# Layer 0's modulation vectors: 32 x 32 block transposes on VectorE and four column-tiled products in place of four TensorE transposes

## The chip, the cores and the metric

One core of a Trainium2 chip runs the whole program, in one launch. The metric is the device time in microseconds; smaller is better. Three runs of the kernel before took 3101.84, 3100.47 and 3102.82 us, median 3101.84.

## The reference

Two transformer layers of width 2048 work on 256 latent tokens and 256 context tokens in fp32. Layer 0 mixes tokens by four pooling windows, layer 1 by neighbourhood attention; both have a gated feed-forward part with a three-tap convolution. Every sub-layer is modulated by vectors that come from one row vector each for the latents (`c`) and the context (`c_ctx`):

```
silu_c, silu_cc = jax.nn.silu(c), jax.nn.silu(c_ctx)
for i in range(DEPTH):
    ml = (silu_c @ w_mod[i] + b_mod[i]).reshape(B, 6, 1, D)
    mc = (silu_cc @ w_mod[i] + b_mod[i]).reshape(6, 1, 1, D)
    a_lat = modulate(rms_norm(h, norm1_g[i]), ml[:, 0], ml[:, 1])
    ...
    h = h + ml[:, 2] * y_lat
    h = h + ml[:, 5] * conv_ffn(modulate(rms_norm(h, norm2_g[i]), ml[:, 3], ml[:, 4]),
                                ffn_w_gate[i], ffn_w_up[i], ffn_conv_w[i], ffn_conv_b[i], ffn_w_down[i])
```

`w_mod` is 2048 x 12288 per layer: a large weight for a product with two rows.

## The kernel before

Channels lie on partitions and tokens along the free axis. A large product is taken three times in a one-pass fp32 form: weights and activations are each split into a high and a low part (ACT rounds, DVE subtracts, L143 and L145), and PE adds high x high, high x low and low x high.

**Layer 0's modulation (`mod_pe`, L187 to L206).** The 12288 columns are 24 chunks of 512. A chunk is loaded in four pieces of 1 MB, two tiles each (L192, issued at L127 on SP's queue). For a piece, four products (L193) with 32-column weights `sc` stand at the four column positions of the array, `tile_position=(0, 32 * j)`, and all 16 of a chunk add up in the one PSUM bank of tag `m`. Then position j holds a quarter of the sum over input channels for both streams, as rows, and it must become columns with the four quarters added: ACT copies the bank to `modev` (L198), PE turns it by four 128 x 128 transposes against `ident` into a bank of tag `d` (L203, tile `modt`, under high priority), DVE adds the four quarters (L205, via the view `by_row`), and `finish_mod` adds the bias (L181) and, for scales, the norm's gain (L183).

**The late shift (`partial`, L514 to L569).** In layer 0 the feed-forward products of the first eight column tiles are begun per channel group g before the second norm is known. What the shift vector adds to them is computed from the same weight tiles by small column-tiled products (L528, tiles `pwg` and `pwu`, 16 sets of eight), which also come out as rows and are turned the same way: ACT copy `peg`/`peu` (L532), four transposes `ptg`/`ptu` (L561), a DVE reduction (L564 or L568) and, for g > 0, an addition into `wsh` (L569).

**What sets the order.** The Python text gives dependencies and priorities; a scheduler in the build places the instructions of each engine's queue by its own timeline, so that pieces of a chunk are spread among the feed-forward products of `partial` (L545 to L547, tiles `cg` and `cu`) and of the pooling mixer (L484 to L486, tile `pm`). `need` and `between` only say when a piece is written down. Each engine then works through its queue strictly in order. Loads take turns in a ring of tiles (`stage`): six of its own, and more that `lend` adds or takes away. The bank of tag `m` exists once, so chunk n + 1 cannot begin before chunk n's bank has been read; tag `d` has three.

The whole of this lies in the first 455 us. Later, layer 1's vectors are made on DVE (`mod_pairs`), which already uses 32 x 32 block transposes from SBUF (L251) and the constant `quad` (four stacked 32 x 32 identities, four times side by side).

Of the kernel before, what the change touches and what calls it, by code (L numbers as in the profile page):

```python
# [10 lines left out]
F32 = mybir.dt.float32  # L11
F32R = mybir.dt.float32r
AF = mybir.ActivationFunctionType
ALU = mybir.AluOpType
AX = mybir.AxisListType
PSUM = bass.MemoryType.PSUM

P = 128
# [39 lines left out]
def kernel(ctx: ExitStack, tc: tile.TileContext, xT, cxT, wmod, wg, wu, wd, wp,  # L58
                         wq, wv, wo, vec, cc, rope, inv, strips, out):
    nc = tc.nc  # L60
    main = ctx.enter_context(tc.tile_pool(name="main", bufs=1))
# [30 lines left out]
    ident = main.tile([P, P], F32, name="ident")  # L92
# [61 lines left out]

    both = (0, 1)

    def by_row(ps):

        return ps.rearrange("p (i j c) -> p i c j", i=4, j=4)[:, :, 0:2, :]

    def quarter_sum(x, n, name):

# [5 lines left out]

    def finish_mod(l, ch, streams, src):

        mt = src[0] if len(src) == 1 else main.tile([P, 4, 2], F32, name=f"modT{l}_{ch}")
        n = len(streams)
        which, q = divmod(ch, 4)

        def dup(name, a):
            return V(name)[:, a : a + 8].rearrange("p (i s) -> p i s", s=2)[:, :, 0:n]

        bias = dup(f"bm_{l}", 8 * ch)
        for b, v in enumerate(src):
            own = slice(32 * b, 32 * b + 32) if len(src) > 1 else slice(0, P)  # L180
            nc.vector.tensor_tensor(mt[own, :, 0:n], v, bias[own], op=ALU.add)  # L181
        if which in (1, 4):
            nc.vector.scalar_tensor_tensor(mt[:, :, 0:n], mt[:, :, 0:n], 1.0, dup(f"g{1 if which == 1 else 2}_{l}", 8 * q),  # L183
                                           op0=ALU.add, op1=ALU.mult)
        modT[l, ch] = mt

    def mod_pe(l, ch, sc, pool):  # L187

        ps = bank("m", f"mod{l}_{ch}")
        for g in range(4):  # L190
            ts = load(lambda a, b: wmod[l, ch, g, :, a:b], 2048, f"wm{l}_{ch}_{g}")
            for j in range(4):  # L192
                nc.tensor.matmul(ps[32 * j : 32 * j + 32, :], sc[:, 4 * g + j, :],  # L193
                                 ts[j // 2][0][:, 512 * (j % 2) : 512 * (j % 2) + 512],
                                 start=(g == 0), stop=(g == 3), tile_position=(0, 32 * j))
            if g == 3:
                ev = pool.tile([P, 512], F32, tag="t2", name=f"modev{l}_{ch}")
                nc.scalar.copy(ev, ps)  # L198
            yield
        with tc.high_priority():  # L200
            p2 = bank("d", f"modt{l}_{ch}")
            for i in range(4):
                nc.tensor.transpose(p2[:, P * i : P * i + P], ev[:, P * i : P * i + P], ident)  # L203
        r = main.tile([P, 4, 2], F32, name=f"modT{l}_{ch}")
        nc.vector.tensor_reduce(out=r, in_=by_row(p2), axis=AX.X, op=ALU.add)  # L205
        finish_mod(l, ch, both, [r])  # L206

    def mod_pairs(todo, ring):

# [113 lines left out]
    with ExitStack() as ph0:  # L323
# [62 lines left out]
        with ExitStack() as phs:  # L386
# [123 lines left out]
            def partial(g, sh, between):  # L510

                step = 0
                for fa in range(0, NS, 4):
                    for q, (nm, wsrc) in enumerate((("g", wg), ("u", wu))):  # L514
# [3 lines left out]
                        for j in range(4):  # L518
                            f = fa + j
                            between(2 * step)  # L520
                            if j == (3 if fa == 0 and q == 0 else 0):
                                need(20 * g + 21)
                                assert g in READY
                                pw = bank("d", f"pw{nm}{g}_{fa}")
                                for i in range(4):
                                    for jj, (t, n) in enumerate(ts):
                                        t3 = t.rearrange("p (f c) -> p f c", c=512)
                                        nc.tensor.matmul(pw[32 * i : 32 * i + 32, 256 * jj : 256 * jj + 256], sh[:, i, :],  # L528
                                                         t3[:, :, P * i : P * i + P], start=True, stop=True,
                                                         tile_position=(0, 32 * i))  # L530
                                ev = f0.tile([P, 512], F32, tag="t2", name=f"pe{nm}{g}_{fa}")
                                nc.scalar.copy(ev, pw)  # L532
                            if f >= NC:
                                if g == 0:
                                    HELD[f, q] = bank("gu", f"c{nm}_{f}")
                                ps = HELD[f, q]
                                first, final = g == 0, g == 3
                            else:
                                ps = bank("d", f"c{nm}{g}_{f}")
                                first = final = True  # L540
                            hi, lo = parts[j // 2]
                            for i in range(4):
                                c = 512 * (j % 2) + P * i
                                xh, xl = flat(A[4 * g + i][:, 0]), flat(A[4 * g + i][:, 1])
                                nc.tensor.matmul(ps, hi[:, c : c + P], xh, start=(first and i == 0), stop=False)  # L545
                                nc.tensor.matmul(ps, hi[:, c : c + P], xl, start=False, stop=False)
                                nc.tensor.matmul(ps, lo[:, c : c + P], xh, start=False, stop=(final and i == 3))  # L547
                                if i == 1:
                                    between(2 * step + 1)
                            step += 1  # L550
                            if f >= NC:
                                continue
                            if g == 0:
                                if q == 0:
                                    PART[f] = act_tile(f"part{f}", F32)
                                nc.scalar.copy(PART[f][:, q], ps)
                            else:
                                nc.vector.tensor_tensor(PART[f][:, q], PART[f][:, q], ps, op=ALU.add)
                        p2 = bank("d", f"pt{nm}{g}_{fa}")
                        for i in range(4):  # L560
                            nc.tensor.transpose(p2[:, P * i : P * i + P], ev[:, P * i : P * i + P], ident)  # L561
                        w_ = wsh[:, q, fa : fa + 4, :]
                        if g == 0:
                            nc.vector.tensor_reduce(out=w_, in_=by_row(p2), axis=AX.X, op=ALU.add)  # L564
                            continue
                        t_ = f0.tile([P, 512], F32, tag="t2", name=f"pu{nm}{g}_{fa}")[:, 0:8]
                        t_ = t_.rearrange("p (f s) -> p f s", s=2)
                        nc.vector.tensor_reduce(out=t_, in_=by_row(p2), axis=AX.X, op=ALU.add)  # L568
                        nc.vector.tensor_tensor(w_, w_, t_, op=ALU.add)  # L569
            lend(range(4, KT))  # L570
            mix = mixer(0)
            for n in STEPS:
# [659 lines left out]
```

## Time and profile before

| what | before |
|---|---|
| runs | 3101.84 us median (3100.47 to 3102.82) |
| the profiled execution's own time | 3103.48 us |
| its span | 3101.7 us (1.8 us lie around it) |
| PE, DVE, ACT, POOL busy | 98%, 62%, 44%, 27% |
| HBM | 180 GB/s mean, 376 and 333 GB/s in the first two of 40 slices |
| layer 0's modulation and late shift | 19.7 to 455 us |
| their instructions that the change touches | 40 ACT copies, 160 transposes, 40 reductions, 12 additions |

The profile counts an engine as busy while an instruction of it is in flight, and matmuls overlap each other, so a busy PE says only that PE had no hole. A group of rows gives the busy time of all, the mean of one, and the idle time just before. In a timeline row the first number is the start, the second the length up to the end of the row's last instruction; the next row's start tells when the next one went in. An fp32 product has two rows in the trace, one for each of its passes: four products at L193 are eight records.

### The profile page before, as it was taken

To read this page: it belongs to the slowest core of one execution; us is meant where nothing else is said; L and a number is where in the kernel's file an instruction comes from. 1 tells how busy PE (TensorE), PEld (TensorE's weight loads), DVE (VectorE), ACT (ScalarE), POOL (GpSimd) and SP (SyncE) were. 2 spreads that over 40 slices of the span, in tenths; PEclk is the share of its full clock that TensorE was granted. 3 is DMA by queue.
4 is the path that set the end of the run, shared out by engine and by line. 5 is a ranking of instruction groups with operands and counts; after the bars stand their busy time and mean duration, and the time that the engine had idled before them with its cause. 6 is when DMAs were issued, how large, how long until landed. Compare 5 with 4: busy or idle time off the path is not lost.

```text
span 3101.7 us, 40819 instructions
## 1 busy us (share of the span) xinstructions
PE 3030.0 (98%) x15082; PEld 2414.3 (78%) x15082; DVE 1932.6 (62%) x2748; ACT 1373.2 (44%) x2219; POOL 826.1 (27%) x823
## 2 busy tenths in 40 slices
PE   6999899999999999999999999999999999999998
PEld 2565558888888888888888788878788888888887
DVE  4445674285765848567485665564777666666666
ACT  3333454333233332323334444343545666656665
POOL 2011213213031230302213000000002466556665
PEclk9999999999999999999999999999999999999999
DMA  9978573264846657475573333332345565555563
GB/s 376 333 271 306 177 246 102 89 217 149 251 141 206 198 162 247 133 225 171 182 226 118 102 113 106 102 114 96 111 153 179 177 196 188 192 189 185 179 195 117
DMA packets 177927, 559.70 MB, mean 180 GB/s; under 512 B 17600, under 2 KB 22208, under 8 KB 177728
## 3 DMA queue, kind: packets, MB, share of 16 engines
q1 hardware_dynamic: 177728, 557.10, 55.0%
q8 instruction: 119, 1.95, 0.3%
q14 instruction: 80, 0.66, 0.1%
HBM read 554.93 MB, written 2.10 MB: 180 GB/s over the span
## 4 chain that ended last, share of the span: by engine, by line
PE 94%; DMA 2%; DVE 2%; POOL 1%; ACT 1%; issue 0%; SPq 0%; DVEq 0%; ACTq 0%; POOLq 0%
PE g L766 5%; PE u L766 5%; PE d L657 5%; PE d L659 5%; PE d L658 5%; PE d L813 4%; PE u L631 4%; PE u L632 4%; PE u L633 4%; PE g L631 4%; PE g L633 4%; PE g L632 4%; PE mod L193 3%; PE u L769 3%; PE g L769 3%; PE d L817 2%
## 5 line engine op out<-in xcount | busy, mean ns | idle before, releaser
L670 POOL TENSOR_TENSOR hl<-hl,dy 128x256 f32<-128x256 f32 x160 | 149.0, 931 | 958.6 <-ACT dy L669 957.3
L828 POOL TENSOR_TENSOR hl<-hl,dy 128x256 f32<-128x256 f32 x320 | 331.5, 1069 | 188.4 <-ACT dy L826 186.1
L241 DVE SCALAR_TENSOR_TENSOR macc<-wm,sc,macc 128x512 f32<-128x512 f32 (+1 forms) x360 | 325.2, 935 | 68.6 <-DMA wm<-wmod 67.6
L669 ACT ACTIVATE dy<-d,modT 128x256 f32<-128x256 f32 x320 | 133.5, 470 | 196.8 <-PE d L659 195.5
L193 PE MATMUL mod<-wm,sc 128*32 128x512 f32 x768 | 134.6, 618 | 26.6 <-DMA wm<-wmod 26.5
L670 POOL TENSOR_TENSOR hc<-hc,dy 128x256 f32<-128x256 f32 x160 | 126.0, 787 | 0.0
L145 DVE TENSOR_TENSOR wd_2l<-wd,wd_2h 128x1024 fp32r<-128x1024 f32 (+1 forms) x44 | 53.9, 1229 | 112.8 <-ACT wd_2h L143 112.8
L826 ACT ACTIVATE dy<-d,modT 128x512 f32<-128x512 f32 x160 | 104.4, 683 | 42.7 <-PE d L817 41.2
L915 POOL TENSOR_TENSOR rk<-rk,rp 128x256 f32<-128x256 f32 x16 | 13.2, 826 | 365.4 <-DVE rk L914 309.8
L145 DVE TENSOR_TENSOR wd_3l<-wd,wd_3h 128x1024 fp32r<-128x1024 f32 (+1 forms) x44 | 52.0, 1202 | 80.6 <-ACT wd_3h L143 80.6
L145 DVE TENSOR_TENSOR wd_1l<-wd,wd_1h 128x1024 fp32r<-128x1024 f32 (+1 forms) x44 | 53.7, 1224 | 58.6 <-ACT wd_1h L143 58.6
L466 POOL TENSOR_TENSOR pf<-ws,inv 128x256 f32<-128x256 f32 x32 | 27.7, 886 | 222.4 <-DVE ws L461 154.7
L193 PEld LDWEIGHTS mod<-wm,sc 128*32 128x32 f32 x768 | 23.6, 110 | 81.0 <-issue 59.4
L143 ACT CAST wd_1h<-wd 128x1024 fp32r<-128x1024 f32 (+1 forms) x44 | 45.2, 1029 | 79.8 <-PE u L632 50.6
L145 DVE TENSOR_TENSOR wd_0l<-wd,wd_0h 128x1024 fp32r<-128x1024 f32 (+1 forms) x44 | 54.6, 1247 | 40.7 <-ACT wd_0h L143 40.6
L1004 ACT ACTIVATE sb<-sb,nm 128x512 f32<-128x512 f32 x64 | 46.1, 721 | 64.4 <-DVE nm L1000 63.2
L143 ACT CAST wd_0h<-wd 128x1024 fp32r<-128x1024 f32 (+1 forms) x44 | 45.3, 1031 | 57.9 <-PE u L766 29.1
L792 DVE TENSOR_TENSOR actb<-sgb,actb 128x256 fp32r<-128x256 f32 x43 | 52.3, 1216 | 27.0 <-ACT actb L791 27.0
L657 PE MATMUL d<-act,wd_2h 128*128 128x512 f32 x172 | 68.0, 395 | 0.0
L658 PE MATMUL d<-act,wd_2h 128*128 128x512 f32 x172 | 67.9, 395 | 0.0
L657 PE MATMUL d<-act,wd_3h 128*128 128x512 f32 x172 | 67.9, 395 | 0.0
L657 PE MATMUL d<-act,wd_0h 128*128 128x512 f32 x172 | 67.9, 395 | 0.0
(1752 smaller groups left out, 9286.1 us busy)
## 6 DMA issues: line engine op xcount, KB each, us to landing
wm<-wmod SPq DMA_DIRECT2D x384, 512.0 KB, 6.1
wd<-wd SPq DMA_DIRECT2D x168, 512.0 KB, 4.4
wg<-wg SPq DMA_DIRECT2D x156, 512.0 KB, 4.6
wu<-wu SPq DMA_DIRECT2D x156, 512.0 KB, 4.5
wv<-wv SPq DMA_DIRECT2D x32, 512.0 KB, 3.9
wk<-wq SPq DMA_DIRECT2D x32, 512.0 KB, 4.0
wq<-wq SPq DMA_DIRECT2D x32, 512.0 KB, 3.7
wo<-wo SPq DMA_DIRECT2D x32, 512.0 KB, 4.4
```

The costliest lines, as they stand in the source:

```text
L145: eng.tensor_tensor(lo[:, :n], t[:, :n], hi[:, :n].bitcast(F32), op=ALU.subtract)
L193: nc.tensor.matmul(ps[32 * j : 32 * j + 32, :], sc[:, 4 * g + j, :], ts[j // 2][0][:, 512 * (j % 2) : 512 * (j % 2) + 512], start=(g == 0) ...
L241: nc.vector.scalar_tensor_tensor(acc[s], v, sc2[:, k, s : s + 1], acc[s], op0=ALU.mult, op1=ALU.add)
L631: nc.tensor.matmul(ps, hi[:, c : c + P], xh, start=(k == 0), stop=False)
L632: nc.tensor.matmul(ps, hi[:, c : c + P], xl, start=False, stop=False)
L633: nc.tensor.matmul(ps, lo[:, c : c + P], xh, start=False, stop=(k == KT - 1))
L657: nc.tensor.matmul(ps, hi[:, o : o + P], xh, start=(i == 0), stop=False)
L658: nc.tensor.matmul(ps, hi[:, o : o + P], xl, start=False, stop=False)
L670: nc.gpsimd.tensor_tensor(h_of(s)[:, k, :], h_of(s)[:, k, :], y[:, s], op=ALU.add)
L766: nc.tensor.matmul(ps, hi[:, c : c + P], flat(B[k]), start=(k == 0), stop=False)
L769: nc.tensor.matmul(ps[:, T:], lo[:, c : c + P], B[k][:, 0], start=False, stop=(k == KT - 1))
L828: nc.gpsimd.tensor_tensor(hl[:, k, :], hl[:, k, :], y[:, q], op=ALU.add)
```

## The change

Both turns are made another way. `turned` lets DVE read the PSUM bank itself and turn its sixteen times four 32 x 32 blocks by one instruction (`nc.vector.transpose` on 128 x 512), so the ACT copy goes. After that the two wanted rows of a quarter are columns on the quarter's own 32 partitions, one block of 32 channels behind the other, in SBUF. `by_row` adds the four quarters with products against `quad[:, 0:32]`: four of them with 8 columns each (four blocks, two streams), of which the one for block b of every 128 channels stands at column position 32 b. They replace the transposes and the reduction. The bias is added by DVE straight from that PSUM bank; for the late shift DVE copies it or adds it to `wsh`. The high priority of the turn is gone. Besides, `mod_pe` writes the products of pieces 0 and 1 down together after the load of piece 1, and those of 2 and 3 after the load of piece 3: eight in a row in the text.

```
+    def turned(ps, pool, name):
+        t = pool.tile([P, 512], F32, tag="t2", name=name)
+        nc.vector.transpose(t, ps)
+        return t.rearrange("p (i b r) -> p b i r", b=4, r=32)[:, :, :, 0:2]
+
+    def by_row(x, name):
+        ps = bank("d", f"{name}s")[:, 0:8].rearrange("p (i s) -> p i s", s=2)
+        for b in range(4):
+            nc.tensor.matmul(ps[32 * b : 32 * b + 32], quad[:, 0:32], x[:, b], start=True, stop=True,
+                             tile_position=(0, 32 * b))
+        return ps
...
-            for j in range(4):
-                nc.tensor.matmul(ps[32 * j : 32 * j + 32, :], sc[:, 4 * g + j, :],
-                                 ts[j // 2][0][:, 512 * (j % 2) : 512 * (j % 2) + 512],
-                                 start=(g == 0), stop=(g == 3), tile_position=(0, 32 * j))
+            if g % 2 == 0:
+                t0 = ts
+            for k, tt in () if g % 2 == 0 else ((g - 1, t0), (g, ts)):
+                for j in range(4):
+                    nc.tensor.matmul(ps[32 * j : 32 * j + 32, :], sc[:, 4 * k + j, :],
+                                     tt[j // 2][0][:, 512 * (j % 2) : 512 * (j % 2) + 512],
+                                     start=(k == 0), stop=(k == 3), tile_position=(0, 32 * j))
             if g == 3:
-                ev = pool.tile([P, 512], F32, tag="t2", name=f"modev{l}_{ch}")
-                nc.scalar.copy(ev, ps)
+                x = turned(ps, pool, f"modev{l}_{ch}")
             yield
-        with tc.high_priority():
-            p2 = bank("d", f"modt{l}_{ch}")
-            for i in range(4):
-                nc.tensor.transpose(p2[:, P * i : P * i + P], ev[:, P * i : P * i + P], ident)
-        r = main.tile([P, 4, 2], F32, name=f"modT{l}_{ch}")
-        nc.vector.tensor_reduce(out=r, in_=by_row(p2), axis=AX.X, op=ALU.add)
-        finish_mod(l, ch, both, [r])
+        finish_mod(l, ch, both, [by_row(x, f"modt{l}_{ch}")])
...
-                                ev = f0.tile([P, 512], F32, tag="t2", name=f"pe{nm}{g}_{fa}")
-                                nc.scalar.copy(ev, pw)
+                                x = turned(pw, f0, f"pe{nm}{g}_{fa}")
...
-                        p2 = bank("d", f"pt{nm}{g}_{fa}")
-                        for i in range(4):
-                            nc.tensor.transpose(p2[:, P * i : P * i + P], ev[:, P * i : P * i + P], ident)
-                        w_ = wsh[:, q, fa : fa + 4, :]
+                        w_, v = wsh[:, q, fa : fa + 4, :], by_row(x, f"pt{nm}{g}_{fa}")
                         if g == 0:
-                            nc.vector.tensor_reduce(out=w_, in_=by_row(p2), axis=AX.X, op=ALU.add)
-                            continue
-                        t_ = f0.tile([P, 512], F32, tag="t2", name=f"pu{nm}{g}_{fa}")[:, 0:8]
-                        t_ = t_.rearrange("p (f s) -> p f s", s=2)
-                        nc.vector.tensor_reduce(out=t_, in_=by_row(p2), axis=AX.X, op=ALU.add)
-                        nc.vector.tensor_tensor(w_, w_, t_, op=ALU.add)
+                            nc.vector.tensor_copy(w_, v)
+                        else:
+                            nc.vector.tensor_tensor(w_, w_, v, op=ALU.add)
```

Three places show what the scheduler makes of it. In the names, `mod_9` and `wm_9_2_0` are chunk 9 and its piece 2 (columns 0 or 1024), the last number is a buffer's; lines of the changed kernel differ by a few (L206 is the old L193, L160 the block transpose, L167 the four small products, L191 the old L181).

The first is PE's queue at the last two pieces of chunk 9, among products of `partial`. Before:

```order
L193 MATMUL mod_9_897<-wm_9_2_0_956,sc 32x512 x2
L546 MATMUL cg_964<-Ad_567,wcg_4h_866 128x512
L547 MATMUL cg_964<-Ad_567,wcg_4l_867 128x512
L545 MATMUL cg_964<-Ad_572,wcg_4h_866 128x512
L193 MATMUL mod_9_897<-wm_9_2_1024_958,sc 32x512 x2
```

and now:

```order
L206 MATMUL mod_9_890<-wm_9_2_0_949,sc 32x512 x2
L206 MATMUL mod_9_890<-wm_9_2_1024_951,sc 32x512 x2
L550 MATMUL cg_995<-Ad_559,wcg_4h_860 128x512
L206 MATMUL mod_9_890<-wm_9_3_0_981,sc 32x512 x2
L551 MATMUL cg_995<-Ad_559,wcg_4h_860 128x512
```

Piece 2 now stands together, but pieces 2 and 3, eight products in the text, are still apart, and piece 3 is split. Over the whole queue up to the first L631 the column-tiled products stand in 95 unbroken runs before and in 85 now. The 384 products of L193 need 122 sets of up to four different column positions before and 126 now; 96 would do if every four stood together.

The second is DVE's queue at the end of chunk 8, the chunk before the first mixer's products. Before:

```order
L461 TENSOR_TENSOR ws_369<-pad_200 128x2x271
L470 TENSOR_TENSOR ph_361<-pf_357,ph_361 128x512
L467 TENSOR_TENSOR pf_371<-pf_371,pad_200 128x512
L205 TENSOR_REDUCE modT_8_405<-modt_8_400 128x8
L181 TENSOR_TENSOR modT_8_405<-modT_8_405,vt 128x8
```

and now:

```order
L467 TENSOR_TENSOR ws_363<-pad_200 128x2x271
L145 TENSOR_TENSOR wp0l_381<-wp_1024_374,wp0h_380 128x1024
L476 TENSOR_TENSOR ph_355<-pf_351,ph_355 128x512
L473 TENSOR_TENSOR pf_365<-pf_365,pad_200 128x512
L160 STREAM_TRANSPOSE modev_8_396<-mod_8_291 128x512
L476 TENSOR_TENSOR ph_369<-pf_365,ph_369 128x512
L191 TENSOR_TENSOR modT_8_403<-modt_8s,vt 128x8
```

What reads the bank of chunk 8 was a copy on ACT; it is now on DVE, behind the fourth `pf` (L467 before, L473 now).

The third is DVE's queue at the end of chunk 10, in the third mixer. Before:

```order
L461 TENSOR_TENSOR ws_1720<-ws_1720 128x2x265
L453 SCALAR_TENSOR_TENSOR py_1770<-hl,modT_6_1639,rs_194 128x256
L453 SCALAR_TENSOR_TENSOR py_1770<-hc,modT_6_1639,rs_194 128x256
L145 TENSOR_TENSOR wp2l_1863<-wp_1024_1856,wp2h_1862 128x1024
L205 TENSOR_REDUCE modT_10_1758<-modt_10_1753 128x8
```

and now:

```order
L467 TENSOR_TENSOR ws_1700<-ws_1700 128x2x265
L145 TENSOR_TENSOR wp2l_1844<-wp_1024_1837,wp2h_1843 128x1024
L160 STREAM_TRANSPOSE modev_10_1729<-mod_10_1627 128x512
L459 SCALAR_TENSOR_TENSOR py_1749<-hl,modT_6_1624,rs_194 128x256
L459 SCALAR_TENSOR_TENSOR py_1749<-hc,modT_6_1624,rs_194 128x256
```

The block transpose stands behind both splits of `wp2`, and the pair `py` has gone behind it.

More of the change, by code (lines that the diff above doesn't have):

```diff
@@ L155 @@
     both = (0, 1)
-    def by_row(ps):
-        return ps.rearrange("p (i j c) -> p i c j", i=4, j=4)[:, :, 0:2, :]
+    def turned(ps, pool, name):
[8 more added lines that the diff above has]
+        return ps
     def quarter_sum(x, n, name):
@@ L169, in finish_mod @@
     def finish_mod(l, ch, streams, src):
-        mt = src[0] if len(src) == 1 else main.tile([P, 4, 2], F32, name=f"modT{l}_{ch}")
+        mt = main.tile([P, 4, 2], F32, name=f"modT{l}_{ch}")
         n = len(streams)
```

## Prediction

> **What bounds the kernel now.** First the page: which engine has no holes, and what the chain that ended last is made of.
>
> ```profile
> span 3101.7 us, 40819 instructions
> PE 3030.0 (98%) x15082; PEld 2414.3 (78%) x15082; DVE 1932.6 (62%) x2748; ACT 1373.2 (44%) x2219; POOL 826.1 (27%) x823
> ...
> PE 94%; DMA 2%; DVE 2%; POOL 1%; ACT 1%; issue 0%; SPq 0%; DVEq 0%; ACTq 0%; POOLq 0%
> ```
>
> PE sets the end. Whatever shortens PE's queue before its last layer-0 shift is kept to the end, since behind it the work is the same. Next, the windows (us, then busy time of PE, PEld, DVE, ACT, POOL, clock, DMA share, GB/s) for the stretch in which the changed instructions lie:
>
> ```profile
> 20.00:60.00 40.00, 31.39 (x133) 9.77 (x130) 19.41 (x40) 10.46 (x18) 7.73 (x9) 0.91 1.03 408
> 60.00:100.00 40.00, 38.55 (x201) 20.52 (x200) 12.61 (x23) 17.59 (x34) 5.68 (x8) 1.00 0.97 350
> 100.00:350.00 250.00, 248.47 (x1392) 152.65 (x1391) 130.49 (x221) 91.13 (x160) 40.73 (x47) 1.00 0.77 278
> 350.00:455.00 105.00, 93.40 (x460) 48.42 (x459) 66.74 (x124) 45.16 (x87) 19.73 (x15) 0.97 0.70 240
> ```
>
> Up to 60 us the loads bound (408 GB/s, DMA share 1.03); from 60 to 350 us PE has 3 us of holes in 290; behind that 11.6 us in 105. DVE has time left everywhere, on the mean. So the change is worth what it takes from PE's own queue, plus or minus holes.
>
> **What it removes from PE.** The timeline of PE gives the prices:
>
> ```profile
> 167.56 0.60 PE L203 MATMUL modt<-ident,modev 128*128 128x128 f32 x4
> 168.09 1.92 PE L193 MATMUL mod<-wm,sc 128*32 128x512 f32 x16
> 169.95 0.66 PE L561 MATMUL ptu<-ident,peu 128*128 128x128 f32 x4
> 170.53 1.92 PE L193 MATMUL mod<-wm,sc 128*32 128x512 f32 x16
> ...
> 196.24 0.39 PE L546 MATMUL cu<-Ad,wcu_0h 128*128 128x512 f32 x1
> 196.47 0.39 PE L547 MATMUL cu<-Ad,wcu_0l 128*128 128x512 f32 x1
> 196.79 1.05 PE L193 MATMUL mod<-wm,sc 128*32 128x512 f32 x4
> 197.77 0.50 PE L545 MATMUL cg<-Ad,wcg_4h 128*128 128x512 f32 x1
> 198.11 0.39 PE L546 MATMUL cg<-Ad,wcg_4h 128*128 128x512 f32 x1
> ...
> 234.76 1.06 PE L193 MATMUL mod<-wm,sc 128*32 128x512 f32 x8
> ```
>
> A full product goes in every 0.23 us (196.24 to 196.47). Sixteen tiled records take 1.92 us, eight 1.06, and four the same 1.05: so a set costs 0.86 us whether it holds four column positions or two. From 196.47 to 198.11 are 1.64 us; less two full products (0.46) and the set (0.86) leaves 0.32 us for going into the column-tiled form and out again.
>
> Four transposes behind full products put the next set off from 167.56 to 168.09, 0.53 us, of which 0.09 for the way in would be paid anyway (196.47 to 196.79, less 0.23): net 0.44. Between tiled sets they cost 169.95 to 170.53, 0.58, and also end the run: 168.09 to 169.95 is 1.86 for two sets (1.72), so 0.14 more, together 0.72. In PE's order 27 of the 40 bursts follow full products and 13 follow tiled ones: 27 x 0.44 + 13 x 0.72 = **21.3 us removed**.
>
> **What it adds to PE.** Forty bursts of four products with 8 columns, two passes each. No row shows such a burst. The nearest rows:
>
> ```profile
> L528 PEld LDWEIGHTS pwu<-wcu,sh x128: 106/110/178, 100.9 to 435.0; 128*32 128x32 f32 x128
> ...
> 354.63 0.58 PE L289 MATMUL n2s<-ones,n2q 128*128 128x1 f32 x4
> 355.08 0.71 PE L545 MATMUL cg<-Ad,wcg_0h 128*128 128x512 f32 x2
> ...
> 236.34 1.09 PE L528 MATMUL pwu<-wcu,sh 128*32 128x256 f32 x16
> 237.23 1.05 PE L193 MATMUL mod<-wm,sc 128*32 128x512 f32 x6
> ```
>
> One-column products go in every 0.11 us (354.63 to 355.08, four records): they cost their weights' load. A 32-column load takes 0.11 us, four positions at once. One exposed load per burst gives 0.11 us, the lower end. The upper end is a pass of the late shift's products, 0.89 us for four passes of 256 columns (236.34 to 237.23): two passes, 0.44. I take two exposed loads and a little, 0.25: 40 x 0.25 = 10.0 us. Eight-column streams say that it is near the load, not near the 256-column pass.
>
> The Trainium skill (TensorEngine Tiling, "Performance Considerations", Instruction Overhead) speaks against this form: each matmul has about 60 cycles of overhead, so tiling should not lean on a dimension that is already small. By that figure a burst of eight passes is an estimated 8 x 25 ns = 0.2 us, 8.0 in all, and the sum would be 2 us better than mine; no run here shows it yet.
>
> The runs: without transposes the old order would have 82 (95 less 13 that a burst cut in two), the new one has 85, five of them small products alone: 3 x 0.32 = 1.0 us. The sets: 126 for 122, 4 x 0.86 = 3.4 us. So eight in a row is worth nothing; the scheduler splits it as before, a loss of one set in thirty. Added: **14.4 us**. PE's own queue gets **6.9 us** shorter (12.5 at the lower price, 0.7 longer at the upper).
>
> **What it moves to DVE, and who waits.** ACT loses 40 copies, DVE gets 40 block transposes; the trace has them from SBUF only:
>
> ```profile
> L198 ACT COPY modev<-mod x24: 564/585/590, 31.7 to 448.8; 128x512 f32<-128x512 f32 x24
> L251 DVE STREAM_TRANSPOSE modu<-macc x32: 665/686/708, 663.4 to 1687.5; 128x512 f32<-128x512 f32 x32
> L1014 DVE COPY pt<-pT x64: 675/686/693, 1803.6 to 2274.3; 128x512 f32<-128x512 f32 x64
> ```
>
> A DVE copy of that size out of PSUM takes the same 0.69 us as the transpose, so 0.69 it is. The 28 us lie in DVE's free time; but the queue is in order, and PE waits for the transpose. Chunk 8, PE, then DVE:
>
> ```profile
> 55.95 1.11 PE L203 MATMUL modt<-ident,modev 128*128 128x128 f32 x4 [1.08 <-ACT modev L198]
> 56.99 1.92 PE L193 MATMUL mod<-wm,sc 128*32 128x512 f32 x4
> 58.85 0.80 PE L484 MATMUL pm<-ph,wp0h 128*128 128x512 f32 x1
> ```
>
> ```profile
> 58.26 0.69 DVE L467 TENSOR_TENSOR pf<-pf,pad 128x512 f32<-128x512 f32 x1 [1.13 <-POOL pf L466]
> ```
>
> Now the transpose starts when that `pf` ends, 58.95, and ends at 59.64; small products 0.25 and a set of about 1.06 follow, and `pm` starts near 60.95 for 58.85: 2.1 us lost. Behind the bank wait all of chunk 16 and the mixer's products. Chunk 10:
>
> ```profile
> 232.34 0.39 PE L547 MATMUL cu<-Ad,wcu_4l 128*128 128x512 f32 x1
> 234.17 0.66 PE L203 MATMUL modt<-ident,modev 128*128 128x128 f32 x4 [1.44 <-ACT modev L198]
> ```
>
> ```profile
> 234.70 0.48 DVE L453 SCALAR_TENSOR_TENSOR py<-hl,modT,rs 128x256 f32<-128x256 f32 x1
> 235.10 0.96 DVE L453 SCALAR_TENSOR_TENSOR py<-hc,modT,rs 128x256 f32<-128x256 f32 x1
> 235.98 1.75 DVE L145 TENSOR_TENSOR wp2l<-wp,wp2h 128x1024 fp32r<-128x1024 f32 x1
> ```
>
> The transpose follows `wp2l`, which ends at 237.73; the pair `py` before it (1.28 us) has moved behind, and 0.2 us of small DVE work is gone: 236.25 + 0.69 = 236.9 for 234.17, **2.7 us** lost, with the next late shift and chunk 18 queued behind.
>
> Holes that shrink, because an ACT copy stood behind other work of ACT, or a small copy behind other work of DVE; PE, ACT and DVE:
>
> ```profile
> 77.71 0.65 PE L203 MATMUL modt<-ident,modev 128*128 128x128 f32 x4 [1.45 <-ACT modev L198]
> ...
> 368.69 1.09 PE L528 MATMUL pwg<-wcg,sh 128*32 128x256 f32 x16 [1.56 <-ACT A L312]
> ...
> 432.33 0.66 PE L203 MATMUL modt<-ident,modev 128*128 128x128 f32 x4 [1.61 <-ACT modev L198]
> ```
>
> ```profile
> 430.74 1.04 ACT L143 CAST wcu_4h<-wcu 128x1024 fp32r<-128x1024 f32 x1 [7.14 <-DMA wcu<-wu]
> ```
>
> ```profile
> 368.43 0.16 DVE L417 COPY sh<-modT 128x8 f32<-128x8 f32 x1
> 431.82 1.23 DVE L145 TENSOR_TENSOR wcu_4l<-wcu,wcu_4h 128x1024 fp32r<-128x1024 f32 x1 [4.07 <-ACT wcu_4h L143]
> ```
>
> DVE has time at 77 us (12.6 us of work in 40), so the first hole falls to about 0.75 (-0.7). At 432 the copy stood behind a rounding that waited for a load, and DVE is idle (-1.5). At 368.69 the row names ACT, but the last to come was DVE's copy of the shift at 368.43; in the new order it stands ahead of four normalising steps (-1.6), while the diagonal for the second norm goes behind one more addition (+1.0): -0.6. At three mixer ends the transpose has under 0.3 us to spare before its old turn; I allow 1.0. Sum: 2.1 + 2.7 - 0.7 - 1.5 - 0.6 + 1.0 = **3.0 us lost**; ends -2.8 (gains alone) and +6.8 (DVE's losses and a further us, no gain).
>
> Net -6.9 + 3.0 = -3.9 us. The profiled execution took 3103.48 us and would take 3099.6; it lies 1.6 us above the median of the runs, so the median goes from 3101.84 to about **3098**.
>
> **The rivals.**
>
> *Small products cheap, and no new wait* (28%): at 0.11 us a burst PE's queue gains 12.5; with 2 us of holes left, -10.5, **3091 us**. For it: PE's positions run side by side in every tiled row. Against: the two places above, read from the order.
>
> *DVE's queue takes ACT's place as what PE waits for* (14%; slower). DVE is 64% busy from 350 to 455 us, and in each of the four mixers a transpose stands among splits and pooling steps. If 2.7 us are lost not at two but at six places (the other mixers' ends and chunks 20 to 23), 4 x 2.7 = 10.8 more, **3109 us**; it decides once PE's holes before DVE's transposes exceed 7 us plus today's.
>
> *The loads take it back* (in the forecast's range): in the stretches to 60 us and from 350 us PE waits for loads. If what is saved there (about a third of the bursts) is waited off, 2.3 us of the 6.9 go, **3100 us**. Against: between 100 and 350 us loads have a quarter of their time free.
>
> *The change doesn't do what it says*: true of the eight in a row, and priced above.
>
> **How the numbers follow.** A measurement of this kernel can tell about 0.2% (6.2 us) from no change. The forecast's own case, from -6.2 to +6.2 us, holds 57%, the cheap case 28%, the slow one 14%, with a percent for what I have not seen on the faster side: faster 0.29, same 0.57, slower 0.14. The range runs from the cheap price with the holes nearly even (-12, 3090) to the dear price with DVE's losses (-3.9 + 7.6 + 2.3 = +6, 3108).
>
> **What would show it.** Right: block transposes out of PSUM near 0.69 us; bursts of small products that put the next set off by 0.2 to 0.3 us; PE holes of 4 to 5 us behind chunk 8 and about 4 us behind chunk 10, both before the small products; none at chunks 16 and 22; the first L631 about 4 us earlier than 454.5; the same stretch lengths behind it. Wrong: bursts above 0.4 us, a transpose near 1.2 us (POOL beside it), holes before small products in every mixer, or a difference that arises behind 455 us, where the order hardly changes.

## The result, and the profile after

| | before | after |
|---|---|---|
| median of the runs | 3101.84 us (3098.64 to 3107.1, 9 runs) | 3110.72 us (3108.2 to 3113.54, 9 runs) |
| ratio after/before, 95% interval | | 1.0027 (1.0018 to 1.0035) |
| profiled execution: own time, span | 3103.48, 3101.7 us | 3108.2, 3106.4 us |

The kernel became 0.27% slower, some 8.5 us; forecast was 3098, and the range ended at 3108. The profiled execution after lies 2.5 us under its median, that of before 1.6 above, so the two profiles show 4.7 us of the difference; where the rest of it arises no profile shows.

First the page of after, its first rows:

```profile
span 3106.4 us, 41103 instructions
...
PE 3023.7 (97%) x15242; PEld 2407.5 (78%) x15242; DVE 1944.8 (63%) x2752; ACT 1352.2 (44%) x2179; POOL 827.1 (27%) x823
```

PE is busy for 6 us less in a span that is 5 us longer: the work left PE's queue, and more than it came back as holes. Then where: the first product of the feed-forward behind the changed stretch, before (line 631) and after (line 630); each row has the shortest, median and longest product in ns and the first and last start in us:

```profile
L631 PE MATMUL g<-A,wg_8h x2: 395/447/499, 454.5 to 455.3; 128*128 128x512 f32 x2
```

```profile
L630 PE MATMUL g<-A,wg_8h x3: 389/389/497, 458.3 to 459.8; 128*128 128x512 f32 x3
```

The product starts 3.8 us later, where the prediction has it about 4 us earlier. From there to the end it is 2647.2 us before and 2648.1 after, so four fifths of the profiles' difference arises in the first 458 us. The windows of after, to be held against the four of the prediction:

```profile
20.00:60.00 40.00, 28.69 (x142) 7.92 (x138) 21.45 (x40) 8.80 (x15) 8.70 (x9) 0.89 1.03 408
60.00:100.00 40.00, 38.94 (x214) 21.31 (x216) 13.85 (x23) 16.14 (x32) 5.92 (x8) 0.98 0.93 343
100.00:350.00 250.00, 238.31 (x1443) 140.71 (x1436) 134.76 (x220) 70.88 (x120) 33.79 (x40) 0.98 0.77 274
350.00:455.00 105.00, 93.22 (x525) 50.45 (x524) 68.19 (x122) 45.89 (x90) 26.14 (x21) 0.95 0.67 229
```

From 100 to 350 us PE had 1.5 us of holes and a clock of 1.00; now it has 11.7 us of holes and 0.98. The waits of PE from 53 to 460 us, summed by what was waited for (us, times, longest), before and after:

```profile
PE modt L203 <- ACT modev L198: 6.3, 5, 1.6
PE pwu L528 <- DMA wcu<-wu: 5.4, 2, 4.1
PE pwg L528 <- ACT A L312: 1.6, 1, 1.6
PE mod L193 <- DMA wm<-wmod: 1.1, 3, 0.6
PE g L631 <- DVE late L355: 0.9, 1, 0.9
PE n2b L299 <- DVE n2d L297: 0.5, 1, 0.5
```

```profile
PE modt_11s L167 <- DVE modev L160: 5.9, 1, 5.9
PE pwu L534 <- DMA wcu<-wu: 4.8, 2, 3.6
PE modt_10s L167 <- DVE modev L160: 4.7, 1, 4.7
PE modt_8s L167 <- ACT ph L475: 4.5, 1, 4.5
PE n2b L305 <- DVE n2d L303: 2.2, 1, 2.2
PE cg L550 <- ACT Ad L508: 1.4, 1, 1.4
PE mod L206 <- DMA wm<-wmod: 1.2, 2, 1.0
PE modt_19s L167 <- DVE modev L160: 1.0, 1, 1.0
...
```

15.8 us before, 28.7 after with four rows left out (0.9, 0.9, 0.8 and 0.4): 12.9 us more. Three holes make 15.1 us of the 28.7, before the small products of chunks 8, 10 and 11. Before, the turns of the same chunks were waited for 1.1, 1.4 and 0 us; the row of chunk 11's turn before has no bracket:

```profile
323.82 0.49 PE L203 MATMUL modt<-ident,modev 128*128 128x128 f32 x3
```

Loads are waited for no longer than before (6.5 and 6.0 us). At chunk 8 the row names ACT, but what the small product works on is the block transpose, which ends at 58.17, 0.15 us before PE starts. It stands behind a `pf` step, as predicted:

```profile
56.85 0.69 DVE L473 TENSOR_TENSOR pf<-pf,pad 128x512 f32<-128x512 f32 x1 [0.53 <-POOL pf L472]
57.46 0.71 DVE L160 STREAM_TRANSPOSE modev<-mod 128x512 f32<-128x512 f32 x1
```

At chunks 10 and 11, PE's timeline, then DVE's:

```profile
227.09 1.92 PE L206 MATMUL mod<-wm,sc 128*32 128x512 f32 x14
...
239.37 0.30 PE L167 MATMUL modt_10s<-modev,quad 128*32 128x8 f32 x8 [4.73 <-DVE modev L160]
239.47 0.31 PE L167 MATMUL ptg_4s<-peg,quad 128*32 128x8 f32 x8
239.58 1.97 PE L534 MATMUL pwu<-wcu,sh 128*32 128x256 f32 x16
...
331.52 0.29 PE L167 MATMUL modt_11s<-modev,quad 128*32 128x8 f32 x8 [5.91 <-DVE modev L160]
```

```profile
224.50 1.22 DVE L145 TENSOR_TENSOR wcu_4l<-wcu,wcu_4h 128x1024 fp32r<-128x1024 f32 x1 [5.08 <-ACT wcu_4h L143]
...
237.38 1.22 DVE L145 TENSOR_TENSOR wp2l<-wp,wp2h 128x1024 fp32r<-128x1024 f32 x1
238.52 0.71 DVE L160 STREAM_TRANSPOSE modev<-mod 128x512 f32<-128x512 f32 x1
...
328.92 1.22 DVE L145 TENSOR_TENSOR wp3l<-wp,wp3h 128x1024 fp32r<-128x1024 f32 x1
330.06 0.69 DVE L467 TENSOR_TENSOR ws<-ws 128x514 f32<-128x514 f32 x1
330.66 0.71 DVE L160 STREAM_TRANSPOSE modev<-mod 128x512 f32<-128x512 f32 x1
```

Chunk 10's last sets are through PE at 229.0 (first row); its transpose starts at 238.52. DVE had stood idle 5.08 us for a split whose weights came late, and then worked off, without a gap, what was queued in front of the transpose: two splits, two pooling steps, two more splits and some additions. PE had other work until 234.6. At chunk 11 one more addition of the pooling lies in front.

One thing more comes with a hole. Windows of after: the hole, and what follows, at chunks 10 and 11 (the clock is the third number from the right):

```profile
234.70:239.30 4.60, 0.00 (x0) 0.00 (x0) 4.57 (x8) 1.57 (x2) 1.69 (x2) 0.96 0.64 256
239.30:242.00 2.70, 2.63 (x36) 1.50 (x40) 2.70 (x8) 1.53 (x3) 0.56 (x1) 0.50 0.70 194
242.00:245.00 3.00, 3.00 (x20) 1.10 (x13) 3.00 (x7) 0.00 (x0) 0.87 (x2) 0.95 0.66 200
325.60:331.50 5.90, 0.01 (x1) 0.01 (x1) 5.76 (x9) 1.58 (x3) 0.66 (x2) 0.67 0.34 131
331.50:334.00 2.50, 2.48 (x36) 1.46 (x40) 2.50 (x7) 1.44 (x3) 1.01 (x2) 0.50 0.03 7
334.00:337.00 3.00, 3.00 (x19) 1.41 (x12) 2.93 (x7) 0.20 (x1) 0.00 (x0) 0.92 0.59 162
```

PE comes back at half its clock: 2.63 x 0.50 + 3.00 x 0.05 = 1.5 us lost at chunk 10, 2.48 x 0.50 + 3.00 x 0.08 = 1.5 at chunk 11. The row of `pwu` above takes 1.97 us for 1.09 in the prediction's row. The Trainium skill (TensorE: Matmul & The Clock Gate, "Part 1: The HAM clock gate") tells of this: half the clock behind an idle window of about 3.4 us, the full clock behind as much of work. The halving agrees; the runs below show it behind a shorter hole too.

### The profile page after: what moved, and what is told of

The parts are those of the page before. It is cut to its first block, busy times and chain, and to the rows that moved or that the text cites. A ratio compares the mean times of both kernels' runs of the same rounds, so it can differ in the third digit from the quotient of the medians.

```text
span 3106.4 us, 41103 instructions
## 1 busy us (share of the span) xinstructions
PE 3023.7 (97%) x15242; PEld 2407.5 (78%) x15242; DVE 1944.8 (63%) x2752; ACT 1352.2 (44%) x2179; POOL 827.1 (27%) x823
## 3 DMA queue, kind: packets, MB, share of 16 engines
q8 instruction: 120, 1.97, 0.2%
## 4 chain that ended last, share of the span: by engine, by line
PE 93%; DVE 2%; DMA 2%; POOL 1%; ACT 1%; issue 1%; SPq 0%; DVEq 0%; ACTq 0%; POOLq 0%
PE g L765 5%; PE u L765 5%; PE d L656 5%; PE d L658 5%; PE d L657 5%; PE d L812 4%; PE u L630 4%; PE u L631 4%; PE u L632 4%; PE g L630 4%; PE g L632 4%; PE g L631 4%; PE mod L206 3%; PE g L768 3%; PE u L768 3%; PE d L816 2%
## 5 line engine op out<-in xcount | busy, mean ns | idle before, releaser
L206 PE MATMUL mod<-wm,sc 128*32 128x512 f32 x768 | 137.6, 624 | 25.2 <-DMA wm<-wmod 25.2
L914 POOL TENSOR_TENSOR rk<-rk,rp 128x256 f32<-128x256 f32 x16 | 13.2, 826 | 365.3 <-DVE rk L913 309.7
L206 PEld LDWEIGHTS mod<-wm,sc 128*32 128x32 f32 x768 | 26.6, 113 | 80.8 <-issue 60.6
```

What stands on the lines that cost most here:

```text
L206: nc.tensor.matmul(ps[32 * j : 32 * j + 32, :], sc[:, 4 * k + j, :], tt[j // 2][0][:, 512 * (j % 2) : 512 * (j % 2) + 512], start=(k == 0) ...
```

## The experiments

**Theory (the queue):** PE waits for block transposes because of their place in DVE's in-order queue. **Rivals:** eight in a row costs; the small products cost; or PE's shorter queue is waited off by loads and by the chain of the pooling whatever the order. Ratios are to the kernel before, run beside each; 0.1% is 3.1 us.

**f1, four in a row again.** `mod_pe`'s loop as before, all else of the change kept:

```
-            if g % 2 == 0:
-                t0 = ts
-            for k, tt in () if g % 2 == 0 else ((g - 1, t0), (g, ts)):
-                for j in range(4):
...
+            for j in range(4):
...
```

> The changed kernel with the modulation products of layer 0 four in a row again, so the block transposes and small products alone. Queue theory (PE waits for block transposes that stand behind other work in VectorE's in-order queue): the transposes stand at the same places as in the changed kernel, behind pf, wp2l and wp3l, so the three holes of 4 to 6 us at chunks 8, 10 and 11 stay and the time is that of the changed kernel, about 8 us above before, give or take 3. Rival (eight in a row costs: two load pieces are held until four are there): the loss goes, 4 us below before to even.

3108.74 us, 1.0026 (1.0015 to 1.0037): as after. The profiled execution has holes of 5.2, 3.6 and 4.0 us at chunks 8, 10 and 11. The block transposes with their small products give the loss alone.

**f2, eight in a row alone**, on the kernel before.

> The kernel before with eight in a row alone; ScalarE copies and TensorE transposes stay. Queue theory: no transpose on VectorE, so no hole of 4 us before small products or transposes; PE's queue has 125 sets for 122 (+2.6 us) and six runs fewer (-1.9 us), so within 3 us of before. Rival (eight in a row costs): 8 us above before, with longer waits for loads.

3105.2 us, 1.0015 (1.0006 to 1.0024): 4.6 us slower, between the two. PE's own wait for the copy of chunk 10 grew:

```profile
236.88 1.11 PE L206 MATMUL modt<-ident,modev 128*128 128x128 f32 x4 [2.17 <-ACT modev L201]
```

2.17 us for 1.44, and the clock halves behind it (0.91 from 230 to 250 us, for 1.00 before). With the run above: 0.15% alone, nothing on top of the transposes. The two parts don't add up.

**f3, chunks 8, 10 and 11 as before.** ScalarE copy and four transposes for these three, the change for the other 37 bursts:

```
-                x = turned(ps, pool, f"modev{l}_{ch}")
+                if ch in (8, 10, 11):
+                    ev = pool.tile([P, 512], F32, tag="t2", name=f"modev{l}_{ch}")
+                    nc.scalar.copy(ev, ps)
+                else:
+                    x = turned(ps, pool, f"modev{l}_{ch}")
...
```

> The changed kernel with chunks 8, 10 and 11 alone as before (ScalarE copy, four transposes on TensorE); the other 37 bursts stay. Queue theory: the holes 4.5, 4.7 and 5.9 us fall to about 1.1, 1.4 and 0, some 12.5 us; the half clock behind each of them goes, some 2 us each where it is on the path, 5 in all; the three bursts cost 0.5 us more each: 16 us below the changed kernel, about 7 us below before. Rival (the small products or the 37 other block transposes cost the time): within 2 us of the changed kernel.

3102.94 us, 1.0004 (0.9996 to 1.0013): 7 us below after, for 16 expected. The three chunks carry most of the loss, so it isn't the small products. Why half the gain was missing, PE's waits of this run show:

```profile
PE modt L220 <- ACT modev L212: 5.6, 3, 2.6
...
PE cg L563 <- ACT wcg_0h L143: 1.7, 1, 1.7
PE cg L563 <- ACT Ad L521: 1.6, 2, 1.4
```

The copies of chunks 10 and 11 were waited for 2.6 and 2.1 us, not 1.4 and 0: from the rounding of the late `wcu` load to PE's transposes of chunk 10 it is 217.07 to 230.50 us here and 220.50 to 234.17 before, 13.4 and 13.7 us, and PE with less to do in between waits longer. `cg` waits too, for a rounding of its weights (1.7 us) and for the mixer's end (`Ad`), neither of which it did before. So part of the last rival is true as well.

**f4, the splits behind the transpose.** An edge that puts the splits of `wp1` to `wp3` behind the block transpose of their group's chunk:

```
+                        hold[:] = [TURN[f"modev0_{8 + g}"]] if g > 0 else []
                         parts = ld(wp[g], f"wp{g}")
+                        hold.clear()
...
```

> The changed kernel, with the splits of the pooled weights of groups 1 to 3 put behind the block transpose of chunks 9 to 11 in VectorE's queue, nothing else. Queue theory: the transposes of chunks 10 and 11 come two splits (2 x 1.22 us) earlier, the holes fall from 4.7 to 2.3 and from 5.9 to 3.5 us, chunk 8 keeps its 4.5: 4.9 us below the changed kernel, and 2 more for each hole behind which the clock no longer falls to half, so 4 to 2 us above before down to even. Rival (the transpose out of PSUM itself, or the copies' absence, sets the wait, not its place): the holes stay above 4 us and the time within 2 us of the changed kernel.

3104.18 us, 1.0011 (1.0002 to 1.0020): 5 us below after, as expected, but partly by luck: PE's order came out with 122 sets for 126 and 81 column-tiled runs for 85, and by the prediction's prices (0.86 us a set, 0.32 a run) these alone are 4.7 us. What speaks for the theory is the holes, 3.9 us at chunk 10 and 3.2 at chunk 11, where 2.3 and 3.5 were expected. At chunk 10 DVE's queue did get shorter by 2.2 us: from the rounding of the late `wcu` load to the end of the transpose it is 226.21 to 239.84 us, for 223.41 to 239.23 after. But that rounding came later against PE's work, 2.2 us behind the start of chunk 6's small products (223.99) for 0.8 (222.60), and that took 1.4 us of the 2.2 back.

**g1, late shifts alone**, the chunks as before, four in a row.

> The kernel before with block transposes and small products for the 16 late shifts alone; all 24 modulation chunks of layer 0 as before, four in a row. Queue theory: nothing of this kernel waits for a late shift's transpose (none of the changed kernel's holes stands before ptg or ptu), so no new hole; 16 bursts save some 0.5 us each, 8 us, of which up to 3 is waited off at chunks 10 and 11 and in the load-bound stretch near 380 us: 5 to 8 us below before. Rival (PE's shorter queue is waited off by loads and by the pooling chain whatever is done): within 2 us of before.

3102.3 us, 1.0005 (0.9996 to 1.0014): a miss. The profiled execution took 3098.47, as expected, but it is the fastest of 11 that go up to 3108.46. No wait for a late shift's transpose stands in it, but PE's other waits from 53 us on sum to 18.9 us for 15.8 before, in small pieces (chunk 10's copy 1.96 us for 1.44, `n2b` 1.6 for 0.5). What takes the rest of the gain back in the median run this profile can't show.

**g2, chunks alone**, the late shifts as before.

> The changed kernel with the late shifts as before, so block transposes for the 24 modulation chunks alone, eight in a row. Queue theory: the three holes at chunks 8, 10 and 11 and the small ones stay, and the 16 bursts' gain is gone: the changed kernel's time or up to 6 us above it, 8 to 14 us above before. Rival (the late shifts' 16 transposes are what fills VectorE's queue): the holes fall below 3 us and the time is 3 to 6 us below the changed kernel.

3117.16 us, 1.0049 (1.0037 to 1.0062), 15 us above before: the holes (5.4, 6.0 and 5.6 us) stay, and the late shifts' gain is gone. Against the whole change the 16 late bursts are worth 0.22%.

**g3, two splits on GpSimd**: `wcu_4l` of groups 1 and 2, so that 2.4 us less lie in DVE's queue.

```
-                        parts = split(ts, f"wc{nm}{g}_{fa}")
+                        parts = split(ts, f"wc{nm}{g}_{fa}", int(fa == 4 and nm == "u" and g in (1, 2)))
```

> The changed kernel with the two splits wcu_4l of groups 1 and 2 on GpSimd, so that VectorE's queue ahead of the transposes of chunks 10 and 11 is 2.4 us shorter; TensorE's work is the same. Queue theory: the holes at 10 and 11 fall by 2 to 3 us each, and with less time at half clock behind them the kernel is 5 to 8 us below the changed one. Rival (the load of wcu that comes late, not VectorE's queue behind it, sets the end of the hole): the holes stay within 1 us and so does the time.

3109.41 us, 1.0027 (1.0018 to 1.0036): nothing. The holes are 3.5 and 6.4 us. But it doesn't speak for the rival, since the queue did not get shorter. POOL, then DVE:

```profile
317.76 4.74 POOL L145 TENSOR_TENSOR wcu_4l<-wcu,wcu_4h 128x1024 fp32r<-128x1024 f32 x2 [47.37 <-ACT wcu_4h L143]
```

```profile
320.74 2.34 DVE L467 TENSOR_TENSOR ws<-pad 128x542 f32<-128x542 f32 x1 [1.92 <-ACT pad L461]
```

The pooling step took 2.34 us beside POOL's split; in after, without it, the same row has 0.72. Just before it DVE waited 1.92 us for ACT's `pad`. So what left DVE's queue came back in it as a wait and a longer step; on loads the run is inconclusive.

**h1, the transpose first.** The pooling steps of groups 1 to 3 are written later, from the second on, and put behind the transpose (the tuple `STEPS` is (9, 9, 9, 9, 13, 13, 17, 17)):

```
+            LATER = (9, 12, 12, 12, 13, 13, 17, 17)
...
-                todo = [20 * g + 20 + n for n in STEPS] if g < 3 else []
+                todo = [20 * g + 20 + n for n in LATER] if g < 3 else []
```

The explicit edges of this run turned out to change no engine's order: the tuple alone gives the same program order.

> The changed kernel, with the pooling steps of groups 1 to 3 from their second input tile on, and the splits of the pooled weights, put behind the block transpose of chunks 9 to 11 in VectorE's queue (the steps are written two half pieces later for that); TensorE's products, VectorE's work and the loads are the same in number. Queue theory: the transposes of chunks 10 and 11 end before TensorE runs out of other work, so the holes of 4.7 and 5.9 us fall below 1 us and the half clock behind them goes; chunk 8 keeps its hole: 8 to 12 us below the changed kernel if nothing is waited off later, 4 to 8 if the mixers' later end costs waits before cg and pm; so 3099 to 3106. Rival (TensorE's shorter queue is waited off by loads and the pooling chain whatever the order): holes of 3 us or more appear elsewhere and the time is within 3 us of the changed kernel's 3110.

3094.49 us, 0.9982 (0.9973 to 0.9991): 14 us below after, and below before. DVE, then PE:

```profile
232.74 0.70 DVE L473 TENSOR_TENSOR ws<-ws 128x530 f32<-128x530 f32 x1
233.35 0.71 DVE L162 STREAM_TRANSPOSE modev<-mod 128x512 f32<-128x512 f32 x1
```

```profile
236.09 0.25 PE L169 MATMUL modt_10s<-modev,quad 128*32 128x8 f32 x8
...
236.24 1.08 PE L542 MATMUL pwu<-wcu,sh 128*32 128x256 f32 x16
```

The transpose is done at 234.06, two us before PE asks for it; the bracket of idle time is gone, and `pwu` takes 1.08 us again. The windows that held the two holes:

```profile
230.00:250.00 20.00, 20.00 (x130) 12.95 (x124) 19.92 (x34) 8.13 (x14) 5.61 (x6) 1.00 0.97 365
325.00:345.00 20.00, 20.00 (x112) 13.22 (x112) 17.01 (x29) 5.79 (x9) 4.68 (x6) 1.00 0.51 173
```

No hole, and a clock of 1.00. PE's waits in the stretch sum to 20.2 us for 28.7. PE's order also has 121 sets for 126, which is 4.3 us by the prediction's 0.86; that part of the 14 is not the transposes' place. (Sets and changes of form are counted in the program order.)

**h2, chunk 8 as before as well**, otherwise h1.

> The kernel of the run before, with chunk 8 as before the change as well (ScalarE copy, four transposes on TensorE). Queue theory: chunk 8's hole falls from 4.5 to about 1.1 us, for 0.5 us more on TensorE, so 3 us below the run before, 3096 to 3103, and if below 3101.8 the first version that beats the kernel before. Rival (the loads bound up to 60 us, and what chunk 8 does is waited off there): within 1.5 us of the run before.

3086.49 us, 0.9951 (0.9937 to 0.9964): 15 us below before and the fastest kernel of this study. Chunk 8's hole is 0.83 us for 5.20. It is 8 us below the run before where 3 were expected. For more than 3 speak 4.4 us of hole, the clock behind it (1.00 from 60 to 100 us, 0.95 in h1) and 6 pairs of changes between tiled and full form fewer in PE's order (1.9 us by 0.32 a pair); against it a new wait of 1.6 us before `cg` and a clock of 0.81 for 1.00 from 345 to 380 us. But the two profiled executions, the slowest of h2 and the fastest of h1, lie only 1.0 us apart, so where the 8 us between the medians arise isn't shown.

**k1, the later pooling steps alone?** The kernel before with the same tuple.

> The kernel before, with only the times at which the mixers' pooling steps are written changed (9, 12, 12, 12, 13, 13, 17, 17 for 9, 9, 9, 9, 13, 13, 17, 17, groups 1 to 3), ScalarE copies and TensorE transposes as before. Queue theory: the kernel before waits 1.44 us at chunk 10 for its copy and nothing at chunk 11, so there is little to free: 0 to 3 us below before. Rival (the later pooling steps are worth the 15 us by themselves, and the block transposes nothing): 8 us or more below before.

3112.89 us, 1.0034 (1.0022 to 1.0046): 11 us slower, where up to 3 us faster was expected. PE's waits, the rows that before hasn't or has smaller:

```profile
PE cg L546 <- ACT pz L492: 2.1, 3, 0.9
PE n2b L299 <- DVE n2d L297: 1.8, 1, 1.8
...
PE cg L547 <- DVE Ad L504: 1.5, 1, 1.5
PE cg L546 <- ACT Ad L503: 1.1, 1, 1.1
```

With the mixer's steps later its end is waited for, 4.7 us before `cg`, with a clock of 0.94 and 0.89 in the 40 us from 250 us on (1.00 before); the rest of the 11 us no row shows. So by themselves the later steps are a price here, not a gain; they paid where a block transpose stands in their queue.

**k2, h2 with four in a row**, and **k3, late shifts alone with the steps later**:

> Run h2 with the modulation products four in a row instead of eight (its order on every engine comes out the same with and without the explicit edges of h1 and h2, so they are left out). If eight in a row is worth nothing on its own, as the first run of four in a row had it: within 3 us of h2, about 15 us below before. Rival (eight in a row pays now that the holes are gone: 11 pairs of changes of form fewer at 0.3 us, 3 sets fewer at 0.86): 5 to 7 us above h2, 8 to 10 below before.

3093.72 us, 0.9973 (0.9961 to 0.9985): 7 us above h2, though the two intervals touch. Its rival fits: once the holes are gone, eight in a row pays, by 3 sets and 11 pairs of changes of form fewer, 6.1 us by their prices.

> Block transposes for the 16 late shifts alone, eight in a row, chunks by ScalarE copy and TensorE transposes, pooling steps written later. Queue theory: 16 of 40 bursts save some 0.5 us each, sets fall to 117, no hole of 2 us: 8 to 11 us below before, and above h2 by what the 23 chunks' bursts are worth, 4 to 8 us. Rival (with the holes gone the chunks' block transposes are worth nothing more, VectorE's longer queue taking it back): within 2 us of h2.

3098.96 us, 0.9995 (0.9986 to 1.0004): 12 us above h2, which has 39 of the 40 bursts changed. Against before it is a miss, as g1 was: 8 to 11 us were expected, and the interval holds no change at all. PE's waits in its profile sum to 20.1 us, for 15.8 before and 17.2 in h2. The chunks' block transposes are worth more than the 4 to 8 us expected, once nothing waits for them; an estimate from the prediction's 21.2 us for 40 bursts and 0.08 us for the small products is 23 x 0.45 = 10.4 us.

## Why the prediction was wrong, point by point

- **PE's own queue: right in kind, too small.** From 53 us to the first feed-forward product PE took, waits aside, 454.5 - 53 - 15.8 = 385.7 us before and 458.3 - 53 - 28.7 = 376.6 after: 9.1 us less, though some of it ran at half clock, and 1.1 us of it because PE was further on at 53 us (chunk 8's last products end at 53.77 us, for 54.87 before). The forecast was 6.9 (27 x 0.44 + 13 x 0.72 is 21.2 and not 21.3, which changes nothing). The mis-sized term is the burst of small products, 0.25 us taken between bounds of 0.11 and 0.44. The rows 239.37, 239.47, 239.58, at half clock, put it at 0.10 and 0.11; h1's rows 236.09, 236.18, 236.24, in a window with a clock of 1.00, at 0.09 and 0.06, below the lower bound. The Trainium skill (TensorEngine Tiling (Array Packing), "Performance Considerations", Instruction Overhead), weighed there at an estimated 0.2 us a burst, is two to three times too dear: the rows of eight records end 0.30 or 0.25 us after they start, but the next burst starts 0.10 or less after.
- **The holes: the step that failed.** "Sum: 2.1 + 2.7 - 0.7 - 1.5 - 0.6 + 1.0 = 3.0 us lost" was 12.9. (Its 2.1 for chunk 8 is the delay of `pm`; the hole itself was to grow by 59.64 - 55.95 = 3.7 us, so it is 4.6 that stands against 12.9.) Its single rows held where it had worked them out. Chunk 10's transpose stands behind `wp2l`, takes 0.71 us for 0.69, and its hole is 4.73 us ("about 4"); chunk 8's is 4.5 ("4 to 5"); chunk 16 has 0.9 for 1.45, chunk 22 0.4 for 1.61; the hole of `pwg` is gone and that of `n2b` 1.6 larger (1.0 expected). But chunk 11, which waited for nothing before, got the largest hole. The prediction looked at its old turn alone ("under 0.3 us to spare ... I allow 1.0"), when the change puts it behind `wp3l` and a pooling step exactly as chunk 10 behind `wp2l`. The hole there was 5.9 us, where 1.0 was allowed for three mixer ends together, and 3.3 more were missing at chunk 19 (1.0) and twice before `cg` (1.4 and 0.9).
- **The clock: not in the sum at all.** Behind each of the long holes PE ran at half clock, 1.5 us lost each time at chunks 10 and 11. A hole's price is its length and this.
- **The rival that came true** is the second: DVE's queue in ACT's place, 3109 us, at 14%. It had the right mechanism and sum, but spread over six places at 2.7; three places hold it, so that its sum came out is in part luck. Its turning point (7 us more before DVE's transposes) was passed.
- **Loads** took nothing more than before from PE directly in after's profile, but a late `wcu` load sets when DVE's queue in front of the transposes of chunks 10 and 11 begins to move. Experiment f3 shows that some of PE's gain is waited off behind that load even where the three chunks are turned on PE; in g1 it is half a microsecond at chunk 10. The prediction priced this at 2.3 us and counted it out between 100 and 350 us.
- **Eight in a row worth nothing**: so it is on top of the transposes (f1), but not by itself: 4.6 us dearer on the kernel before, 7 us cheaper once the holes are gone. By the counts of sets and changes of form it acts through the order that comes out, not through PE's price of a product.
- **Behind 458 us** the difference is 0.9 us, as foreseen near nothing.

What stays open: why g1 and k3 gain nothing in their medians; where h2's last 8 us arise; and the last microseconds of PE's queue. With the burst at 0.06 to 0.09 the prediction's terms give 13.2 to 14.4 us (21.2 - 4.4 less 40 bursts). Measured are 8.0 (9.1 less the 1.1 that PE was ahead) and what the half clock hides: by the windows behind 60 us 0.02 x 38.9 + 0.02 x 238.3 + 0.05 x 93.2 = 10.2 us after and 0.03 x 93.4 = 2.8 before, 7.4 more at most, since part of it falls into the holes. So the gain lies between 8.0 and 15.4, which holds the terms' sum; no run narrows it further.

## What to carry to other kernels

A result that another engine waits for should not be moved to an engine because that engine is idle on the mean: look up what stands in front of it in the in-order queue at every place of the same kind, also where nothing waits today. When it was moved, write the work that has time (here the pooling steps) behind it; the same change was then 0.18% faster than before (5.6 us), and 0.49% (15 us) with one chunk left on ScalarE, instead of 8.5 us slower. Price a PE hole of two us or more with the slower clock that can follow it.

## What the runs showed of the hardware

- The granted clock fell to 0.50 for some 3 us behind holes of 4.7 and 5.9 us, and also behind one of 2.17 us (f2: 0.91 over 230 to 250 us). Before's holes of 1.44 and 1.45 us left it at 1.00. The length alone doesn't settle it: in f3 a hole of 2.13 us left it at 1.00, and one of 1.71 us, 4 us behind one of 0.99, was followed by 0.50. The idle window of about 3.4 us that the Trainium skill gives (TensorE: Matmul & The Clock Gate, "Part 1: The HAM clock gate"), read as a least length of a hole, is thus too long here.
- A block transpose of 128 x 512 fp32 on DVE out of PSUM took 716 ns in the median, for 686 out of SBUF (the row of L251 in the prediction):

```profile
L160 DVE STREAM_TRANSPOSE modev<-mod x24: 701/716/719, 32.1 to 455.4; 128x512 f32<-128x512 f32 x24
```

- Column-tiled products with 8 columns in fp32 held up the next column-tiled products by 0.06 to 0.09 us per burst of four at a clock of 1.00 (h1), and by 0.10 to 0.11 at 0.50, though each record lasts 0.17 to 0.20 us.
- A DVE addition of 542 columns took 2.34 us beside a POOL subtraction of 1024 columns (g3), for 0.72 alone (after).
